# Attention with values as the stationary operand, and probabilities divided ahead of their transposes

## The chip, the cores and the metric

The kernel runs on one core of one Trainium2 chip. The metric is the device time of one execution in microseconds (us). The kernel before takes 1104.72 us, the median of three runs (1103.87 to 1105.32).

## The reference

A trunk of two layers over one sequence of 256 tokens of width 1024, in float32. Each layer is a feed-forward part, a token mixer and a second feed-forward part. Each part normalises its input, applies a shift and a scale, and adds its output times a gate; shift, scale and gate come from a conditioning vector through a large matrix (`ada_w`). The mixer of the first layer is attention with 16 heads, that of the second a state-space scan. The change lies in the attention:

```python
def one_block(args):
    q_blk, i = args
    s = jnp.einsum('bhqd,bhkd->bhqk', q_blk, kt) * scale
    q_pos = i * Q_BLOCK + jnp.arange(Q_BLOCK)
    s = jnp.where(k_pos[None, :] <= q_pos[:, None], s, -jnp.inf)
    p = jax.nn.softmax(s, axis=-1).astype(vt.dtype)
    return jnp.einsum('bhqk,bhkd->bhqd', p, vt)
```

Queries come in two blocks of 128 tokens, heads have 96 features for scores and 64 for values. The 16 results are joined to 1024 features and multiplied by `w_o`.

## The kernel before, in words

**Layout.** The state x lies with features on the 128 partitions (eight chunks of 128) and the 256 tokens along the free axis. A projection multiplies 128x128 pieces of weights (stationary) with 128x256 of tokens (moving). Weights come from HBM in float32 by DMAs of at most 2048 columns (`prefetch`, L171, issued on SP, five buffers `raw`). `split_next` (L200) splits each piece of 1024 columns into a high part (ScalarE, L197) and a low part (VectorE, L198), five pieces being held at most; `mm3` (L282) then does three passes of the rounded type fp32r. Every TensorE matmul is recorded at L272, every transpose at L277.

**The conditioning matrix.** `ada_w` comes over the same DMA queue, between the weights, in units of 1 MB. `plan` (L108) writes the order of all loads; `ADA_AT` says how many units lie in each of five parts (first feed-forward, attention, second, third, scan). `ada_half` (L229) takes the next loaded half unit, multiplies and sums it on VectorE (L236) and frees the buffer after the second half; it is called at fixed places (a call does nothing when no unit is loaded), and by `advance` when all buffers hold such units. The down projection (`down`, L442) of a feed-forward part calls it twice per output chunk.

**Attention** (`mla`, L693). The queries of each four heads (a quad) are projected, squared, rotated and transposed while earlier heads are being worked on. `turn(t)` (L947) works on several heads at once:

- `scores` (L869) of head t: the second block of queries against 256 keys and the first against 128, in plain float32, each followed by a bf16 matmul that adds the mask.
- `softmax` of head t-1: two maxima on VectorE (L887, L888), a small product (L889), two exponentials on ScalarE with their sums (L892).
- `probs_t` of head t-2: three 128x128 transposes on TensorE; `probs_evac` of head t-3 copies them to SBUF (VectorE L908, for one head in four ScalarE L906).
- `values` of head t-4: three float32 matmuls with the transposed probabilities stationary and 64 columns of values moving, so that the output has tokens on partitions.
- once per quad: `o_evac` divides by the sums (VectorE, L925 and L927), `o_t` transposes the result back to features on partitions (four transposes), `o_split` splits it (ScalarE L197, VectorE L198) for the projection by `w_o`.

Turns 0 to 18 stand ahead of that projection; turns 19 to 22 are called between the first pieces of it (`down`, two output chunks early, a hook after each two of the eight inputs).

**Order.** The program is handed to a planner (`tc`), which orders the instructions of each engine by its own costs and by what is ready in its plan; program order is kept only where `keep_in_program_order` says so. On the chip each engine then runs its list in that order.

## Time and profile before

| | us |
|---|---|
| median of the runs | 1104.72 |
| profiled execution | 1103.92 |
| its span | 1102.2 |
| TensorE busy | 1078.9 |
| VectorE busy | 864.9 |
| ScalarE busy | 610.7 |

The span is the stretch that the profile covers; the execution's own time is 1.72 us longer. A record of a matmul is longer than the distance to the next one, since matmuls are pipelined: the distance of two starts is what one costs. Attention with its turns lies from about 262 to 310 us.

### The profile page before, as it was taken

The page shows a single profiled execution, that of the slowest core. Times are in us where ns is not written, and L with a number is a line of the kernel's source. Part 1 is how long each engine was busy: PE and PEld are TensorE (multiplying, and loading weights), DVE is VectorE, ACT ScalarE, POOL GpSimd, SP SyncE. Part 2 cuts the span into 40 slices and gives each one's busy share as a digit, 9 for nine tenths or more (in the row PEclk, how much of TensorE's full clock was granted, in tenths as well). Part 3 has the DMA queues.
Part 4 walks back from the last instruction along what each step waited for, and adds up shares of the span by engine and source line. Part 5 has one row for each costly group of instructions (what it writes and reads, how often), then busy time and mean ns, then how long its engine had stood idle before and what let it go on. Part 6 is the DMA issues. An engine that isn't in the chain of part 4 may idle for free.

```text
span 1102.2 us, 21874 instructions
## 1 busy us (share of the span) xinstructions
PE 1078.9 (98%) x8890; PEld 1064.4 (97%) x8890; DVE 864.9 (78%) x1537; ACT 610.7 (55%) x1081; POOL 48.5 (4%) x107
## 2 busy tenths in 40 slices
PE   4999999999999999999999999999999999999998
PEld 3999999998999999999999999999999999999998
DVE  5889898789879988765999886598887777756642
ACT  4555444468757544444754444498678556544431
POOL 3000020010000000000000000000100100000000
PEclk9999999999999999999999999999999999999999
DMA  8988998755146888775689986544424355666630
GB/s 350 346 330 307 363 358 326 255 202 187 39 162 242 303 328 294 283 263 192 230 326 365 351 321 250 174 149 155 151 98 153 115 192 176 219 222 224 235 130 20
DMA packets 37400, 258.54 MB, mean 235 GB/s; under 512 B 4274, under 2 KB 5426, under 8 KB 6708
## 3 DMA queue, kind: packets, MB, share of 16 engines
q1 hardware_dynamic: 37300, 257.16, 63.7%
q8 instruction: 69, 1.13, 0.4%
q14 instruction: 31, 0.25, 0.1%
HBM read 256.10 MB, written 1.05 MB: 233 GB/s over the span
## 4 chain that ended last, share of the span: by engine, by line
PE 94%; DVE 2%; DMA 1%; ACT 1%; issue 1%; POOL 0%; SPq 0%; POOLq 0%; ACTq 0%
PE bank L272 93%; PE bank L277 2%; DMA raw<-in_adaw_dram 1%; DVE raw L236 1%; DVE wlo L198 1%; ACT whi L197 0%; ACT t L892 0%; DVE sl L307 0%; POOL t L1312 0%; SPq L328 0%; POOL sl L557 0%; POOL rr L415 0%; DVE sl L1230 0%; SPq L178 0%; DVE mod L250 0%
## 5 line engine op out<-in xcount | busy, mean ns | idle before, releaser
L272 PE MATMUL bank<-sl,whi 128*128 128x256 f32 (+1 forms) x5312 | 953.7, 283 | 4.5 <-ACT whi L197 4.5
L272 PEld LDWEIGHTS bank<-sl,whi 128*128 128x128 f32 x5312 | 815.9, 188 | 6.1 <-ACT whi L197 5.0
L272 PE MATMUL bank<-sl,wlo 128*128 128x256 f32 (+1 forms) x2656 | 746.6, 281 | 6.3 <-DVE wlo L198 6.2
L197 ACT CAST whi<-raw 128x1024 fp32r<-128x1024 f32 (+1 forms) x342 | 354.7, 1041 | 362.5 <-PE bank L272 261.7
L272 PEld LDWEIGHTS bank<-sl,wlo 128*128 128x128 f32 x2656 | 501.5, 189 | 7.2 <-DVE wlo L198 7.0
L198 DVE TENSOR_TENSOR wlo<-raw,whi 128x1024 fp32r<-128x1024 f32 (+1 forms) x342 | 412.9, 1212 | 118.2 <-ACT whi L197 116.5
L236 DVE SCALAR_TENSOR_TENSOR raw<-raw,cb 128x1024 f32<-128x1024 f32 x144 | 174.3, 1222 | 20.9 <-DMA raw<-in_adaw_dram 20.8
L306 ACT CAST sl<-t 128x256 fp32r<-128x256 f32 x125 | 48.9, 401 | 21.4 <-DVE t L490 15.5
L307 DVE TENSOR_TENSOR sl<-t,sl 128x256 fp32r<-128x256 f32 x125 | 51.3, 417 | 0.6 <-ACT sl L306 0.5
L435 DVE SCALAR_TENSOR_TENSOR x<-bank,mod,x 128x256 f32<-128x256 f32 x48 | 22.9, 480 | 28.1 <-PE bank L272 28.1
L490 DVE TENSOR_TENSOR t<-t,bank 128x256 f32<-128x256 f32 x70 | 29.2, 417 | 15.4 <-PE bank L272 15.4
L272 PE MATMUL bank<-sl,sl 128*128 128x64 f32 (+3 forms) x264 | 40.2, 291 | 0.0
L272 PEld LDWEIGHTS bank<-sl,sl 128*128 128x128 f32 (+1 forms) x264 | 34.4, 191 | 2.8 <-issue 0.5
L1035 DVE SCALAR_TENSOR_TENSOR sl<-t,cst,sl 128x256 f32<-128x256 f32 x72 | 35.4, 494 | 1.1 <-ACT sl L1033 0.6
L385 ACT ACTIVATE sl<-x,scol 128x256 fp32r<-128x256 f32 x40 | 20.3, 508 | 21.9 <-DVE x L435 21.7
L384 POOL CAST sl<-bspl 128x4 fp32r<-128x4 f32 x40 | 16.1, 446 | 303.8 <-PE bank L272 134.5
L489 ACT ACTIVATE t<-bank 128x256 f32<-128x256 f32 x70 | 26.3, 378 | 0.0
L415 POOL TENSOR_TENSOR rr<-rv,mhalf 128x2 f32<-128x2 f32 x12 | 10.9, 911 | 311.8 <-DVE rv L411 297.7
L272 PE MATMUL bank<-whi,sl 128*128 128x384 f32 (+1 forms) x80 | 24.3, 369 | 0.0
L386 DVE SCALAR_TENSOR_TENSOR sl<-x,scol,sl 128x256 fp32r<-128x256 f32 x40 | 19.1, 480 | 4.8 <-ACT sl L385 4.8
L398 ACT ACTIVATE t<-t,mod,scol 128x256 f32<-128x256 f32 x32 | 18.3, 596 | 6.7 <-DVE t L397 6.7
L1157 ACT ACTIVATE sl<-bank,nac 128x128 f32<-128x128 f32 x64 | 18.3, 373 | 4.3 <-PE bank L272 4.3
(207 smaller groups left out, 611.9 us busy)
## 6 DMA issues: line engine op xcount, KB each, us to landing
raw<-in_wgu_dram SPq DMA_DIRECT2D x88, 1024.0 KB, 5.4
raw<-in_adaw_dram SPq DMA_DIRECT2D x72, 1024.0 KB, 6.9
raw<-in_wdn_dram SPq DMA_DIRECT2D x44, 1024.0 KB, 6.3
raw<-in_win_dram SPq DMA_DIRECT2D x19, 1024.0 KB, 5.0
raw<-in_wout_dram SPq DMA_DIRECT2D x8, 1024.0 KB, 4.8
raw<-in_mwo_dram SPq DMA_DIRECT2D x4, 1024.0 KB, 4.9
raw<-in_mwq_dram SPq DMA_DIRECT2D x3, 768.0 KB, 4.2
raw<-in_mwa_dram SPq DMA_DIRECT2D x2, 1024.0 KB, 7.0
```

The source lines that it names most:

```text
L197: self.nc.scalar.copy(out=hi, in_=raw)
L198: self.nc.vector.tensor_tensor(out=lo, in0=raw, in1=hi.bitcast(F32), op=ALU.subtract)
L236: nc.vector.scalar_tensor_tensor(out=w, in0=w, scalar=1.0, in1=self.cb, op0=ALU.mult, op1=ALU.mult, accum_out=self.mod[:, q, 2 * u + i:2 * ...
L272: ins = self.nc.tensor.matmul(*a, **k)
L277: ins = self.nc.tensor.transpose(*a, **k)
L306: self.nc.scalar.copy(out=hi, in_=src)
L307: self.nc.vector.tensor_tensor(out=lo, in0=src, in1=hi.bitcast(F32), op=ALU.subtract)
L385: nc.scalar.activation(out=hi[:, 0:T], in_=self.x[m], func=AF.Copy, scale=sc)
L435: nc.vector.scalar_tensor_tensor(out=self.x[m], in0=ps[:, 0:T], scalar=self.mod[:, q, m:m + 1], in1=self.x[m], op0=ALU.mult, op1=ALU.add)
L489: nc.scalar.activation(out=tg, in_=pg[:, 0:T], func=AF.Silu)
L490: nc.vector.tensor_tensor(out=tg, in0=tg, in1=pu[:, 0:T], op=ALU.mult)
L1035: nc.vector.scalar_tensor_tensor(out=dst, in0=u[:, t:t + T], scalar=cw[:, t:t + 1], in1=dst, op0=ALU.mult, op1=ALU.add)
```

## The change

- `values` takes a pair of heads. The values (128 tokens by 64 features) are stationary and the transposed probabilities move. The two heads write to partitions 0 to 63 and 64 to 127 of one bank, as features by tokens, 256 columns wide. So `o_evac` and `o_t` go, and `o_split` splits one 128x256 result per pair.
- `norm` is new: as the division can no longer be made on the output, each head's probabilities are divided before their transposes: a reciprocal, a product of 128x256 on VectorE and one of 128x128 on ScalarE.
- `probs_t` puts its three blocks in another order in the bank.
- `scores` adds the mask to both blocks by one matmul of 256 columns.
- `ADA_AT` moves four units (4 MB) from the attention's loads to those of the first feed-forward part, whose down projection calls `ada_half` three times per output chunk.
- The turns end two earlier, at 20; turns 17 to 20 are called inside `down`.

```diff
--- before.py
+++ after.py
@@ -30,7 +30,7 @@
 NDEF = 6
 ZRAW = 13
 SETUP_AT = 15
-ADA_AT = (20, 4, 16, 20, 0)
+ADA_AT = (24, 0, 16, 20, 0)
 BIG_NEG = -1e30
 SSD_ORDER = "ccccczzcz" + "ccczccczz" + "ccczcccz" * 2 + "zzzzzz"
 SSD_STEPS = (1, 1)
@@ -536,7 +536,7 @@
             if not s or j > NDEF:
                 self.ada_half()
             prev = cur
-        self.down(s, NJ, lambda k: H[k], [lambda: evac(prev, None)], 2, 1, 2)
+        self.down(s, NJ, lambda k: H[k], [lambda: evac(prev, None)], 2, 1, 2 if s else 3)
 
     def open_first(self):
 
@@ -864,7 +864,7 @@
         QT[0] = [self.heads_evac(b, None) for b in qb]
         q_evac(1, 1, p1)
 
-        SC, PB, PTs, O, DEN, OT, ON, OB = {}, {}, {}, {}, {}, [], {}, {}
+        SC, PB, PTs, O, DEN, OT = {}, {}, {}, {}, {}, []
 
         def scores(h):
             quad, hh = divmod(h, 4)
@@ -873,14 +873,13 @@
             qt = QT[quad][i][0:96, j * 256:(j + 1) * 256]
             ps = SC[h] = self.bank()
             self.matmul(ps[:, 0:256], qt[:, 128:256], kt, start=True, stop=False)
-            self.matmul(ps[:, 128:256], self.identb, self.maskq, start=False, stop=True)
-            self.matmul(ps[:, 256:384], qt[:, 0:128], kt[:, 0:128], start=True, stop=False)
-            self.matmul(ps[:, 256:384], self.identb, self.maskq, start=False, stop=True)
+            self.matmul(ps[:, 256:384], qt[:, 0:128], kt[:, 0:128], start=False, stop=False)
+            self.matmul(ps[:, 128:384].rearrange("p (c l) -> p c l", c=2), self.identb,
+                        self.maskq.rearrange("p (o l) -> p o l", o=1).broadcast_to([128, 2, 128]),
+                        start=False, stop=True)
 
         def softmax(h):
             quad, hh = divmod(h, 4)
-            if hh == 0:
-                DEN[quad] = self.small([128, 2, 4], "den", 3)
             cq = CQ[quad]
             ps = SC[h]
             mx = self.small([128, 2], "mx", 4)
@@ -888,17 +887,25 @@
             nc.vector.reduce_max(out=mx[:, 0:1], in_=ps[:, 256:384], axis=AX.X)
             nc.vector.scalar_tensor_tensor(out=mx, in0=mx, scalar=-1.0, in1=cq[:, :, hh], op0=ALU.mult, op1=ALU.mult)
             P = self.t3()
+            den = DEN[h] = self.small([128, 2], "den", 4)
             for c, sl in ((1, slice(0, 256)), (0, slice(256, 384))):
                 nc.scalar.activation(out=P[:, sl], in_=ps[:, sl], func=AF.Exp, bias=mx[:, c:c + 1],
-                                     scale=cq[:, c, hh:hh + 1], accum_out=DEN[quad][:, c, hh:hh + 1])
+                                     scale=cq[:, c, hh:hh + 1], accum_out=den[:, c:c + 1])
             SC[h] = P
 
+        def norm(h):
+            P, den = SC[h], DEN.pop(h)
+            nc.vector.reciprocal(out=den, in_=den)
+            nc.vector.tensor_scalar(out=P[:, 0:256], in0=P[:, 0:256], scalar1=den[:, 1:2], scalar2=None, op0=ALU.mult)
+            nc.scalar.activation(out=P[:, 256:384], in_=P[:, 256:384], func=AF.Copy, scale=den[:, 0:1])
+
         def probs_t(h):
+
             P = SC.pop(h)
             pp = PB[h] = self.bank()
             for b in range(3):
-                self.transpose(out=pp[:, b * 128:(b + 1) * 128], in_=P[:, b * 128:(b + 1) * 128],
-                                    identity=self.ident)
+                o = (b + 1) % 3 * 128
+                self.transpose(out=pp[:, o:o + 128], in_=P[:, b * 128:(b + 1) * 128], identity=self.ident)
 
         def probs_evac(h):
             PTs[h] = self.t3()
@@ -907,42 +914,19 @@
             else:
                 nc.vector.tensor_copy(out=PTs[h], in_=PB.pop(h)[:, 0:384])
 
-        def values(h):
-            quad, hh = divmod(h, 4)
-            half, h8 = divmod(h, 8)
-            if hh == 0:
-                O[quad] = self.bank()
-            PT = PTs.pop(h)
-            hc = slice(h8 * 64, (h8 + 1) * 64)
-            o0 = O[quad][:, hh * 64:(hh + 1) * 64]
-            o1 = O[quad][:, 256 + hh * 64:256 + (hh + 1) * 64]
-            self.matmul(o1, PT[:, 0:128], V[0][half][:, hc], start=True, stop=False)
-            self.matmul(o1, PT[:, 128:256], V[1][half][:, hc], start=False, stop=True)
-            self.matmul(o0, PT[:, 256:384], V[0][half][:, hc], start=True, stop=True)
-
-        def o_evac(quad):
-            den = DEN.pop(quad)
-            nc.vector.reciprocal(out=den, in_=den)
-            t = ON[quad] = self.slot()
-            nc.vector.tensor_tensor(
-                out=t.rearrange("p (c h d) -> p c h d", c=2, d=64),
-                in0=O.pop(quad).rearrange("p (c h d) -> p c h d", c=2, d=64),
-                in1=den.rearrange("p c (h o) -> p c h o", o=1).broadcast_to([128, 2, 4, 64]), op=ALU.mult)
-
-        def o_t(quad):
-            t = ON.pop(quad)
-            ps = OB[quad] = self.bank()
-            for b in range(2):
-                for c in range(2):
-                    self.transpose(out=ps[:, b * 256 + c * 128:b * 256 + (c + 1) * 128],
-                                        in_=t[:, c * 256 + b * 128:c * 256 + (b + 1) * 128], identity=self.ident)
-
-        def o_split(quad):
-            ps = OB.pop(quad)
-            hi, lo = self.slot(F32R), self.slot(F32R)
-            self.split_pair(hi, lo, ps)
-            for b in range(2):
-                OT.append((hi[:, b * T:(b + 1) * T], lo[:, b * T:(b + 1) * T]))
+        def values(pair):
+
+            ps = O[pair] = self.bank()
+            hs = [2 * pair, 2 * pair + 1]
+            PT = [PTs.pop(h) for h in hs]
+            for c in range(2):
+                for j, h in enumerate(hs):
+                    half, h8 = divmod(h, 8)
+                    self.matmul(ps[j * 64:(j + 1) * 64, c * 128:T], V[c][half][:, h8 * 64:(h8 + 1) * 64],
+                                PT[j][:, c * 256:256 + c * 128], start=(c == 0), stop=(c == 1))
+
+        def o_split(pair):
+            OT.append(self.split_act(O.pop(pair)[:, 0:T]))
 
         def turn(t):
 
@@ -954,14 +938,14 @@
                     q_rstd(1)
                 if nq < 4:
                     turn.p0 = q_proj(nq, 0)
+            if 0 <= t - 2 < HEADS:
+                norm(t - 2)
             if 0 <= t - 3 < HEADS:
                 probs_evac(t - 3)
             if 0 <= t - 1 < HEADS:
                 softmax(t - 1)
-            if t >= 8 and t % 4 == 0:
-                o_evac(t // 4 - 2)
-            if t >= 10 and t % 4 == 2:
-                o_split(t // 4 - 2)
+            if t >= 6 and t % 2 == 0:
+                o_split(t // 2 - 3)
             if t < HEADS:
                 scores(t)
             if nq < 4:
@@ -974,10 +958,8 @@
                     q_rstd(nq)
             if 0 <= t - 2 < HEADS:
                 probs_t(t - 2)
-            if 0 <= t - 4 < HEADS:
-                values(t - 4)
-            if t >= 9 and t % 4 == 1:
-                o_t(t // 4 - 2)
+            if t >= 5 and t % 2 == 1:
+                values(t // 2 - 2)
             if quad + 1 < 4:
                 if hh == 1:
                     turn.qb = quad_t(QQ[quad + 1])
@@ -986,10 +968,10 @@
             if t % 2 == 1:
                 self.ada_half()
 
-        tail = HEADS + 3
+        tail = HEADS + 1
         for t in range(tail):
             turn(t)
-        rest = [lambda t=t: turn(t) for t in range(tail, HEADS + 7)]
+        rest = [lambda t=t: turn(t) for t in range(tail, HEADS + 5)]
         self.down(s, 8, lambda k: OT[k], rest, 2, 2, 1, MLA_EVERY)
 
 
```

## Rows read from the trace of the kernel before

**Rows 1.** The page, part 1: busy us, share of the span, instructions
```profile
PE 1078.9 (98%) x8890; PEld 1064.4 (97%) x8890; DVE 864.9 (78%) x1537; ACT 610.7 (55%) x1081; POOL 48.5 (4%) x107
```

**Rows 2.** The page, part 4: the chain that ended last, by engine
```profile
PE 94%; DVE 2%; DMA 1%; ACT 1%; issue 1%; POOL 0%; SPq 0%; POOLq 0%; ACTq 0%
```

**Rows 3.** Two windows: length, busy (x instructions) of PE, PEld, DVE, ACT, POOL; clock; DMA share; GB/s
```profile
262.00:274.00 12.00, 10.73 (x72) 9.45 (x71) 11.57 (x48) 9.68 (x27) 0.00 (x0) 1.00 0.67 240
...
262.00:298.00 36.00, 34.69 (x266) 31.46 (x265) 32.21 (x123) 28.89 (x91) 0.20 (x2) 1.00 0.33 118
```

**Rows 4.** Timeline of TensorE for one head: start us, us recorded, engine, line, operation
```profile
295.51 0.60 PE L272 MATMUL bank<-sl,sl 96*128 96x256 f32 x2
295.95 0.22 PE L272 MATMUL bank<-maskq,identb 128*128 128x128 bf16 x1
296.00 0.44 PE L272 MATMUL bank<-sl,sl 96*128 96x128 f32 x2
296.28 0.22 PE L272 MATMUL bank<-maskq,identb 128*128 128x128 bf16 x1
296.34 0.50 PE L277 MATMUL bank<-ident,t 128*128 128x128 f32 x3
296.67 0.78 PE L272 MATMUL bank<-sl,t 128*128 128x64 f32 x6
297.29 0.43 PE L272 MATMUL bank<-sl,sl 96*128 96x256 f32 x1
```

**Rows 5.** The chain of waits, 290 to 330: start us, us, what
```profile
301.10 0.82 PE bank L277 x7
305.17 0.44 PE bank L277 x4
```

**Rows 6.** Groups of VectorE by form: xcount | busy us, mean ns | idle before
```profile
L307 DVE TENSOR_TENSOR sl<-t,sl 128x256 fp32r<-128x256 f32 x125 | 51.3, 417 | 0.6 <-ACT sl L306 0.5
L887 DVE TENSOR_REDUCE mx<-bank 128x1 f32<-128x256 f32 x16 | 6.7, 418 | 2.0 <-PE bank L272 2.0
L888 DVE TENSOR_REDUCE mx<-bank 128x1 f32<-128x128 f32 x16 | 4.5, 280 | 0.0
L198 DVE TENSOR_TENSOR sl<-bank,sl 128x512 fp32r<-128x512 f32 x4 | 2.8, 690 | 2.6 <-ACT sl L197 2.6
L927 DVE TENSOR_TENSOR sl<-bank,den 128x512 f32<-128x512 f32 x4 | 2.8, 689 | 0.8 <-PE bank L272 0.8
L666 DVE TENSOR_SCALAR t<-t,bcol,cst 128x256 f32<-128x256 f32 x5 | 2.0, 410 | 0.0
L925 DVE RECIPROCAL den<-den 128x8 f32<-128x8 f32 x4 | 0.8, 196 | 0.6 <-ACT t L892 0.6
```

**Rows 7.** The groups of VectorE again, 262 to 298 only
```profile
L236 DVE SCALAR_TENSOR_TENSOR raw<-raw,cb 128x1024 f32<-128x1024 f32 x2 | 2.4, 1216 | 0.0
```

**Rows 8.** Groups of ScalarE by form
```profile
L306 ACT CAST sl<-t 128x256 fp32r<-128x256 f32 x125 | 48.9, 401 | 21.4 <-DVE t L490 15.5 <-DVE t L497 5.2 <-DVE t L666 0.5
L892 ACT ACTIVATE t<-bank,mx,cq 128x256 f32<-128x256 f32 x16 | 9.1, 570 | 4.5 <-DVE mx L889 4.5
L892 ACT ACTIVATE t<-bank,mx,cq 128x128 f32<-128x128 f32 x16 | 7.3, 458 | 0.0
L197 ACT CAST sl<-bank 128x512 fp32r<-128x512 f32 x4 | 2.4, 588 | 5.1 <-PE bank L277 5.1
L1180 ACT COPY t<-bank 128x128 f32<-128x128 f32 x4 | 1.0, 257 | 0.0
```

**Rows 9.** The same for 30 to 210, the first feed-forward part
```profile
30.00:210.00 180.00, 178.52 (x1500) 178.25 (x1499) 160.01 (x269) 87.69 (x134) 9.52 (x13) 1.00 0.87 328
```

**Rows 10.** Waits 30 to 222: who waited for whom, us, times, longest
```profile
ACT whi L197 <- PE bank L272: 52.4, 36, 2.4
```

**Rows 11.** Timeline of TensorE where 32-column weights begin
```profile
224.87 0.50 PE L272 MATMUL bank<-ones,ssum 128*128 128x1 f32 x4
225.23 0.41 PE L272 MATMUL bank<-sl,whi 128*32 128x258 f32 x2
```

## The prediction

> **What bounds the kernel now.** I read the page's busy times first. TensorE is busy for 98% of the span [rows 1], and the chain that ended last is TensorE's for 94% [rows 2]; the reader is to see that a microsecond of TensorE's work counts nearly everywhere, and work of other engines only where TensorE waits. The windows come next, since the shares are means. In the attention, 262 to 298, TensorE is busy for 34.69 of 36 us, VectorE for 32.21 and ScalarE for 28.89; nearly all of TensorE's idle time lies in the first 12 us (10.73 of 12), where VectorE is busy for 11.57 [rows 3]. So TensorE is the bound here, but VectorE stands right behind it, and the change takes work from the first and gives it to the second. The timeline of one head in the middle of the attention shows TensorE without a gap, one head in 1.78 us (295.51 to 297.29) [rows 4].
>
> **The change part by part, TensorE.** All costs are distances of two starts.
>
> The transposes of the output go: four per quad, 0.44 us for four [rows 5], four quads, 1.76 us.
>
> The mask. A head's scores take 0.83 us: 0.44 for the float32 pair of passes with 256 columns, 0.05 for a mask, 0.28 for the pair with 128, 0.06 for a mask [rows 4]. After the change the first pair stays at 0.44; the second takes between 0.22 (half of the first) and 0.28; one mask of 256 columns takes the two old ones together, 0.10 to 0.12. That is 0.76 to 0.84, so a head gains 0.07 or loses 0.01. I take 0.04, since the 0.28 holds 0.06 that a pair of 256 doesn't have per column and that I put down to the change of type: 0.6 us over 16 heads, between -0.2 and 1.1. The maxima now wait for the whole of the scores and not for their first part; that is 0.3 us later, a turn ahead of need.
>
> The values. Before, six passes of 64 columns take 0.62 us per head [rows 4], 0.10 each, though the columns alone would need a quarter of the 0.22 that 256 take: loading 128 columns of weights sets this pace, as it does for matmuls of a single column (four in 0.36) [rows 11]. After, a head has two passes of 256 and two of 128: 0.44 plus 0.22 to 0.28, so 0.66 to 0.72. One after the other that is 0.04 to 0.10 more per head. No row shows two matmuls in two halves of the columns. If the second pass of one head ran beside the first of the other, a pair would need 0.88 and not 1.32, a head 0.18 less than before. I take 0.05 more, because it needs only what rows 4 show: 0.8 us, between +1.6 and -2.9.
>
> TensorE in all: 1.76 + 0.6 - 0.8 = 1.6 us less, with ends at 0 and 5.8.
>
> **VectorE and ScalarE.** VectorE gets 16 reciprocals at 0.196, at most (the row has eight columns, the new ones two), 16 products of 128x256 at 0.410, and eight low parts of 128x256 at 0.417: 13.0 us. It loses four reciprocals at 0.196 and four divisions at 0.689, four low parts of 128x512 at 0.690 [rows 6], and two halves of the conditioning matrix at 1.22 [rows 7]: 8.7 us. Net 4.3 more. The nearest row for the product is L666, the same form in SBUF, at 0.410. ScalarE gets 16 products of 128x128, bounded by a plain copy at 0.257 and the exponential at 0.458; I take 0.36, halfway, 5.8 us; and eight high parts at 0.401, less four at 0.588 [rows 8]: 6.6 more.
>
> The row of the product is also where a rule speaks: 128 columns take 0.280 in the maximum and 256 take 0.418 [rows 6], so an element costs about 1.08 ns, and the product's 0.410 is that of a plain pass. The Trainium skill's page "VectorE: DVE Perf Modes", section "The perf-mode tier table (the rule you actually need)", says that a float32 `tensor_scalar` in SBUF runs at twice that rate. By the rule one product would take 0.27, an estimate (0.410 less the 0.138 of 128 columns), and VectorE's addition would be 2.2 us smaller, which would help the first rival below; the row disagrees.
>
> Put together for 262 to 298 [rows 3]: VectorE 32.2 + 4.3 = 36.5, ScalarE 28.9 + 6.6 = 35.5, TensorE 34.7 - 1.6 = 33.1. VectorE then has more work than the stretch is long, while some of its records overlap and the last heads reach past 298. So what TensorE saves inside the stretch is mostly not to be had: VectorE is late next. Past 298 the other engines have room: two of the four transposes of outputs lie there (at 301.10, among seven, and 305.17) [rows 5], 0.88 us, and I count them in full. Of the other 0.7 I count half. The sum is 1.2 us.
>
> **The new wait.** The reciprocal waits on VectorE for ScalarE's sums of the same head; behind it in the written order stand the product, the copy of the transposed probabilities of the head before and the maxima of the next head, for which ScalarE's exponentials wait. ScalarE's product waits for the reciprocal, and the transposes for both products. This ping-pong costs nothing where the planner puts other work between; the third rival has its price.
>
> **The moved loads.** Four units of 1 MB, each with a DMA on SP, two passes of 1.22 on VectorE with the read of their sum, go past the attention's weights into the first feed-forward part. From 30 to 210 us the DMA moves 328 GB/s at a share of 0.87, and VectorE is busy for 160.0 of 180 us [rows 9]. Four MB more in 180 us make 351 GB/s, a share of 0.93; eight passes at 1.3 make VectorE 170.4 at most. Both fit, and the weights are split well ahead: ScalarE waited 36 times, 52.4 us, for TensorE to free a piece [rows 10]. So I cost it at nothing. If that cover were gone, the price, an estimate, would be what a share held at 0.90 leaves over, 0.03 of 180 us, 5.4 us. In the attention the weights' loads come earlier by the same four DMAs, which frees time that the queue doesn't lack (a share of 0.33) [rows 3]. The two turns that move into `down` put the last heads' waits beside its matmuls; before, TensorE had no gap there either, so nothing is counted.
>
> The profiled execution took 1103.92 us, 1.72 over its span; 1.2 less is 1102.7. It lies 0.8 under the median of the runs, 1104.72, so I expect a median of 1103.5.
>
> **The rivals.** First: TensorE stays the bound and the halves run side by side. For it: rows 4 show no gap, and some VectorE records overlap; against it: VectorE's 36.5 us. TensorE would save 1.76 + 0.6 + 2.9 = 5.3; of this 0.88 and 1.1 (six heads past 298 at 0.18) count in full and half of the remaining 3.3, 3.6 in all: 1101.1 us. The Trainium skill's page "TensorEngine Tiling (Array Packing)", section "Key Properties", says that tiles work independently of each other, which would make this the case; no row of before shows it.
>
> Second, to the other side: each turn becomes a loop. If the planner leaves a head's division ahead of the next head's maxima, VectorE's maxima (0.418 + 0.280) are followed by ScalarE's exponentials (0.570 + 0.458), these by the reciprocal and the product (0.196 + 0.410) [rows 6, 8], and only then come the next maxima: 2.33 us, where a head takes 1.78 now. It decides from the point where this order stands in VectorE's list, and over the eight heads that have no query work to fill the gaps it costs 0.55 x 8 = 4.4: 1104.7 - 1.2 + 4.4 = 1107.9. For it speaks that ScalarE already waits for the product of the maxima, 4.5 us in all [rows 8]; against it that the planner reorders by what is ready.
>
> Third: going into and out of half-width weights empties TensorE's pipe. A mask is recorded for 0.22 where the next matmul starts 0.05 later, so an emptied pipe shows 0.17 [rows 4]; 16 times that, twice per pair, is 2.7 us: 1103.5 + 2.7 = 1106.2. Against it: four one-column matmuls, 0.36 us for four, are followed by weights of 32 columns without a gap [rows 11]. The page just named says, in the same section, that a change of the tiling mode empties the engine; the rows disagree as far as 32 columns at the first partition go.
>
> **How the numbers follow.** The forecast, VectorE as the new pace, has a chance of 0.42 and a range of its own of 1102 to 1105. The first rival has 0.28, the loop 0.18, the emptied pipe 0.12. The range reaches from 1100.6 to 1107.2: it leaves out some 0.06 of the first rival, where more than half of the 3.3 is had, and some 0.12 of the loop, where it is whole. Below 0.2%, which is 2.2 us, this kernel's runs can't be told from no change. Faster by more (under 1102.5) is the first rival and a small part of the forecast, 0.36; slower by more (over 1106.9) is the loop, 0.18; the rest, 0.46, is within.
>
> **What would show it.** In the trace after, the transposes of outputs are gone, a head's scores start 0.76 to 0.84 before its next work, and a pair's values take 1.3 (the forecast) or 0.9 (the first rival). VectorE should be busy for 34 us or more of 36 in the attention, and TensorE should have idle time there, ended by VectorE's or ScalarE's products. A wait of the reciprocal for the sums in every turn shows the loop; a gap ahead of each pair's values shows the emptied pipe. TensorE's windows from 30 to 210 should stay full; if they don't, the moved loads were not free and I am wrong there. A product at 0.27 would show that the row of L666 was the wrong one.

## The result, and the profile after

The kernel after takes 1112.68 us, the median of four runs (1110.69 to 1113.21), against 1105.02 for the kernel before beside it: a ratio of 1.0068, with an interval of 1.0054 to 1.0081. That is 7.5 us more. The forecast was 1103.5, its range ended at 1107.2: slower was the side with the smallest chance, and the size was missed. Four things share the time (the moved loads, a wait, the products' work and TensorE's clock); the experiments take them apart. Traced runs with a mean granted clock of 0.998 have a spell at half clock in their opening (39 to 43 us; 0.61 in e1, 1.00 in the kernel before), and a kernel's runs at 0.998 are about 1.5 us longer than its runs at 1.000 (before: 1105.5 and 1104.0), so some comparisons below are made at the same clock.

The page's busy line and its chain of waits of the kernel after answer to [rows 1] and [rows 2]:

```profile
PE 1077.7 (97%) x8826; PEld 1057.7 (95%) x8826; DVE 869.7 (78%) x1565; ACT 614.2 (55%) x1101; POOL 43.4 (4%) x107
...
PE 90%; DVE 5%; ACT 2%; DMA 1%; issue 1%; POOL 0%; SPq 0%; ACTq 0%; POOLq 0%
```

TensorE's busy time hardly moved (1078.9 before), but its share of the chain fell from 94 to 90%, while VectorE's rose from 2 to 5%: TensorE now waits. The windows of the attention, with the columns of [rows 3], and one short window behind it:

```profile
262.00:274.00 12.00, 11.27 (x80) 10.51 (x78) 11.61 (x49) 11.60 (x28) 0.00 (x0) 1.00 0.41 131
262.00:298.00 36.00, 29.94 (x211) 25.57 (x211) 33.27 (x134) 31.51 (x94) 0.00 (x0) 1.00 0.26 88
...
304.00:308.00 4.00, 4.00 (x18) 3.14 (x15) 1.56 (x6) 1.37 (x5) 0.10 (x1) 0.50 0.00 0
```

From 262 to 298 TensorE is busy for 29.94 us and not for 34.69, and yet the attention ends later. From 304 to 308 it shows as full, but at a granted clock of 0.50, that is, at 1.2 and not 2.4 GHz: a busy TensorE is no proof of speed there.

What the engine does when nothing is late shows in its timeline (columns as in [rows 4]):

```profile
281.86 0.49 PE L277 MATMUL bank<-ident,t 128*128 128x128 f32 x3
282.28 0.87 PE L272 MATMUL bank<-t,sl 128*64 128x256 f32 x8
283.08 1.08 PE L277 MATMUL bank<-ident,t 128*96 128x128 f32 x8
...
295.02 0.82 PE L272 MATMUL bank<-sl,sl 96*128 96x256 f32 x4
295.68 0.27 PE L272 MATMUL bank<-maskq,identb 128*128 128x256 bf16 x1
295.79 0.49 PE L277 MATMUL bank<-ident,t 128*128 128x128 f32 x3
296.12 0.82 PE L272 MATMUL bank<-sl,sl 96*128 96x256 f32 x4
...
296.89 0.63 PE L277 MATMUL bank<-ident,t 128*128 128x128 f32 x3
297.44 0.87 PE L272 MATMUL bank<-t,sl 128*64 128x256 f32 x8
298.24 0.92 PE L272 MATMUL bank<-sl,sl 96*128 96x256 f32 x4
```

A head's scores with the mask take 0.77 (295.02 to 295.79; 0.83 before), three transposes 0.33 as before, and the values of two heads 0.80 (297.44 to 298.24; twice 0.62 before): 1.50 a head where it was 1.78. So TensorE has less to do than the forecast thought, and the time is lost in waiting. One place, on all engines (the brackets give the idle time ahead and what ended it):

```profile
302.16 0.34 DVE L899 TENSOR_SCALAR t<-t,den 128x256 f32<-128x256 f32 x1
...
302.49 0.27 DVE L887 TENSOR_REDUCE mx<-bank 128x1 f32<-128x128 f32 x1
...
302.65 0.87 PE L277 MATMUL bank<-ident,t 128*128 128x128 f32 x3 [0.96 <-DVE den L898]
302.68 0.35 DVE L899 TENSOR_SCALAR t<-t,den 128x256 f32<-128x256 f32 x1
303.45 0.30 PEld L272 LDWEIGHTS bank<-t,sl 128*64 128x64 f32 x4 [0.33 <-issue]
303.45 1.55 PE L272 MATMUL bank<-t,sl 128*64 128x256 f32 x8
303.56 0.56 DVE L915 COPY t<-bank 128x384 f32<-128x384 f32 x1 [0.53 <-PE bank L277]
...
304.04 0.15 DVE L888 SCALAR_TENSOR_TENSOR mx<-mx,cq 128x2 f32<-128x2 f32 x1
```

TensorE's transposes wait 0.96 us for the division: they start at 302.65, behind the product of their head (302.16 to 302.50; the trace names the reciprocal that ends next). VectorE's list has the next head's product (L899, 302.68) and the copy (L915) between a later head's maxima (L887) and their small product (L888), which ScalarE's exponentials need; the copy itself waits for the transposes, and these waited for the product of 302.16. At the half clock the same eight passes then take 1.48 us (303.45 to 304.93, where the next scores begin) and not 0.80.

The new instructions, 255 to 325 us (columns as in [rows 6]; VectorE, then ScalarE):

```profile
L899 DVE TENSOR_SCALAR t<-t,den 128x256 f32<-128x256 f32 x16 | 5.6, 347 | 0.1
...
L898 DVE RECIPROCAL den<-den 128x2 f32<-128x2 f32 x16 | 2.5, 158 | 0.9 <-ACT t L892 0.9
...
L900 ACT ACTIVATE t<-t,den 128x128 f32<-128x128 f32 x16 | 6.6, 410 | 3.5 <-DVE den L898 3.3
```

And the moved loads: two windows of the first feed-forward part (columns as in [rows 3]), and the waits from 30 to 222 us (columns as in [rows 10]):

```profile
150.00:180.00 30.00, 29.70 (x252) 29.50 (x252) 26.61 (x40) 13.20 (x19) 4.11 (x6) 1.00 0.93 353
180.00:210.00 30.00, 28.57 (x239) 28.15 (x238) 27.08 (x45) 13.52 (x19) 0.00 (x0) 1.00 0.90 327
```

```profile
ACT sl L385 <- DVE x L435: 28.0, 7, 5.7
...
ACT whi L197 <- PE bank L272: 19.0, 15, 2.6
```

Before, TensorE was full in both windows; the second one was:

```profile
180.00:210.00 30.00, 30.00 (x257) 30.00 (x256) 24.37 (x38) 14.13 (x19) 0.00 (x0) 1.00 0.75 270
```

ScalarE's wait for free weight pieces, which stood for "split well ahead", fell from 52.4 us [rows 10] to 19.0. In its place ScalarE waits 28.0 us, with later splits behind it in its list, for VectorE's sum into x (L435), which waits for TensorE.

### The profile page after: what moved, and what is told of

The parts are those of the page before. It is cut to its first block, busy times and chain, and to the rows that moved or that the text cites. A ratio compares the mean times of both kernels' runs of the same rounds, so it can differ in the third digit from the quotient of the medians.

```text
span 1110.5 us, 21781 instructions
## 1 busy us (share of the span) xinstructions
PE 1077.7 (97%) x8826; PEld 1057.7 (95%) x8826; DVE 869.7 (78%) x1565; ACT 614.2 (55%) x1101; POOL 43.4 (4%) x107
## 4 chain that ended last, share of the span: by engine, by line
PE 90%; DVE 5%; ACT 2%; DMA 1%; issue 1%; POOL 0%; SPq 0%; ACTq 0%; POOLq 0%
PE bank L272 89%; DVE wlo L198 1%; DVE raw L236 1%; PE bank L277 1%; DMA raw<-in_adaw_dram 1%; ACT whi L197 1%; ACT t L892 0%; ACT sl L690 0%; DVE sl L307 0%; DVE t L899 0%; DVE t L915 0%; POOL t L1294 0%; ACT t L813 0%; ACT sl L688 0%; DVE mx L886 0%
## 5 line engine op out<-in xcount | busy, mean ns | idle before, releaser
L435 DVE SCALAR_TENSOR_TENSOR x<-bank,mod,x 128x256 f32<-128x256 f32 x48 | 22.9, 481 | 31.5 <-PE bank L272 31.5
L277 PE MATMUL bank<-ident,t 128*96 128x128 f32 (+2 forms) x116 | 17.9, 285 | 8.5 <-DVE t L899 3.2
L277 PEld LDWEIGHTS bank<-ident,t 128*96 128x96 f32 (+2 forms) x116 | 13.4, 138 | 12.1 <-PE bank L272 4.3
L384 POOL CAST sl<-bspl 128x4 fp32r<-128x4 f32 x40 | 11.1, 322 | 308.5 <-DVE bspl L258 120.5
```

What stands on the lines that cost most here:

```text
L277: ins = self.nc.tensor.transpose(*a, **k)
L435: nc.vector.scalar_tensor_tensor(out=self.x[m], in0=ps[:, 0:T], scalar=self.mod[:, q, m:m + 1], in1=self.x[m], op0=ALU.mult, op1=ALU.add)
```

## The experiments

Ratios are to the kernel before on the same chip, with 95% intervals; 0.0010 is 1.1 us. Each run's record also has its mean granted clock; "at the same clock" compares runs that show the same mean.

### Which half of the change

**e1_ada_only**: the kernel before with the moved loads alone.

```diff
-ADA_AT = (20, 4, 16, 20, 0)
+ADA_AT = (24, 0, 16, 20, 0)
...
-        self.down(s, NJ, lambda k: H[k], [lambda: evac(prev, None)], 2, 1, 2)
+        self.down(s, NJ, lambda k: H[k], [lambda: evac(prev, None)], 2, 1, 2 if s else 3)
```

> The kernel before with the moved loads alone (ADA_AT and three half units per output chunk). Theory A (both parts cost time on their own): 1107 to 1109, with TensorE idle between 170 and 200 us. Theory B (the moved loads carry the whole loss): 1111 or more. If the stretch from 170 to 200 was an accident of the attention's order: 1105.

**e2_attn_only**: the kernel after with these two lines as before.

> The changed attention with the old placing of the loads. Theory A: 1108 to 1110, TensorE idle in the attention as in the changed kernel. Theory B: 1105 or less. The forecast's sum without its moved loads: 1103.8.

**e4_mask_only**: the kernel before with the new mask alone.

```diff
-            self.matmul(ps[:, 128:256], self.identb, self.maskq, start=False, stop=True)
-            self.matmul(ps[:, 256:384], qt[:, 0:128], kt[:, 0:128], start=True, stop=False)
-            self.matmul(ps[:, 256:384], self.identb, self.maskq, start=False, stop=True)
+            self.matmul(ps[:, 256:384], qt[:, 0:128], kt[:, 0:128], start=False, stop=False)
+            self.matmul(ps[:, 128:384].rearrange("p (c l) -> p c l", c=2), self.identb,
+                        self.maskq.rearrange("p (o l) -> p o l", o=1).broadcast_to([128, 2, 128]),
+                        start=False, stop=True)
```

> The kernel before with the one mask matmul of 256 columns alone. By TensorE's records (0.77 instead of 0.83 per head, 16 heads) 1.0 us less: 1104.0. If TensorE isn't what a head waits for: 1105.0. The interval will hardly tell these apart; the trace's distance between a head's scores and its next matmul will.

Measured: e1 1106.8 us, 1.0020 [1.0011, 1.0029]; e2 1110.34 us, 1.0048 [1.0033, 1.0063]; e4 1103.34 us, 0.9988 [0.9978, 0.9997]. The loads cost 2.2 us, the attention 5.3, and these add up to the 7.5 of the whole; the mask alone gains 1.3.

### What the division costs

**e3_no_norm**: e2 without the two products, so the output stays undivided. **e5_norm_tiny**: e2 with the products over two columns, so the same chain of waits with less work; all but these columns stay undivided.

```diff
-            nc.vector.tensor_scalar(out=P[:, 0:256], in0=P[:, 0:256], scalar1=den[:, 1:2], scalar2=None, op0=ALU.mult)
-            nc.scalar.activation(out=P[:, 256:384], in_=P[:, 256:384], func=AF.Copy, scale=den[:, 0:1])
+            nc.vector.tensor_scalar(out=P[:, 0:2], in0=P[:, 0:2], scalar1=den[:, 1:2], scalar2=None, op0=ALU.mult)
+            nc.scalar.activation(out=P[:, 256:258], in_=P[:, 256:258], func=AF.Copy, scale=den[:, 0:1])
```

> As e2, but the two products that divide the probabilities are left out (the reciprocal stays, the output is not divided). If the division's work and its wait hold TensorE back: TensorE without gaps in most of the attention, and its saving of about 6 us comes through, 1098 to 1100. If something else holds it back (banks, order, the pair): within 2 us of e2.

> As e2, but each head's two products take 2 columns instead of 256 and 128 (the rest of the probabilities is not divided): the waits for the sums and for the reciprocal stay, the work goes. Leaving the products out altogether took 7.8 us off e2 (1110.3 to 1102.6). If the added waits cost it: 1108 to 1110. If the products' work on VectorE and ScalarE costs it: 1103 to 1104.

Two columns do not take the work away, as this expects. The groups of e5, 255 to 325 us (columns as in [rows 6]; VectorE, then ScalarE):

```profile
L899 DVE TENSOR_SCALAR t<-t,den 128x2 f32<-128x2 f32 x16 | 3.6, 222 | 0.2
...
L900 ACT ACTIVATE t<-t,den 128x2 f32<-128x2 f32 x16 | 4.9, 304 | 4.3 <-DVE den L898 2.4 <-DVE mx L888 1.9
```

So of 5.6 us of products on VectorE and 6.6 on ScalarE, two columns leave out 2.0 and 1.7.

**e8_deep**: e2 with one turn more between the products and the transposes (and all that follows). **e15_deep_tiny**: e8 with the tiny products of e5.

```diff
-            if 0 <= t - 2 < HEADS:
-                probs_t(t - 2)
+            if 0 <= t - 3 < HEADS:
+                probs_t(t - 3)
...
-        tail = HEADS + 1
+        tail = HEADS + 2
```

> As e2, with the transposes of a head one turn later than its division, and all that follows one turn later too: the same work, one turn more for the products. If TensorE loses time because it reaches the transposes before the products are there: 1104 to 1107. If VectorE and ScalarE simply have too much work: 1109 to 1111.

> The attention's change with old loads and one turn more between the products and the transposes, the products over 2 columns only (the probabilities stay undivided but for these). Full products without the extra turn cost 7.8 us over none, tiny ones 4.1, full ones with the extra turn 3.2. If the cost is a wait of the turn plus the products' own work, and the two add up: 7.8 less 3.7 for the work and 4.6 for the wait leaves nothing, 1102.3 to 1103.0. If the reciprocal's place in VectorE's list costs something whatever comes after it: 1104 to 1105.

| products | no extra turn | an extra turn |
|---|---|---|
| full | e2: 1110.34, 1.0048 [1.0033, 1.0063] | e8: 1105.79, 1.0002 [0.9992, 1.0011] |
| two columns | e5: 1106.67, 1.0019 [1.0009, 1.0028] | e15: 1102.32, 0.9974 [0.9963, 0.9985] |
| none | e3: 1102.56, 0.9984 [0.9975, 0.9994] | |

The division costs 7.8 us (e2 less e3). A turn more takes back 4.4 to 4.6 at either width: that is the wait. The two widths differ by 3.5 to 3.7 at either depth: that is the 2.0 and 1.7 us of work. So these are two costs that add, as e15's first theory had it; e3 and e5 lie outside both of their expected ranges.

The medians mix clocks, though. At a mean clock of 1.000, e3 takes 1102.3, e15 1102.2, e8 1103.9 (two runs each) and e5 1104.5 (one run); at 0.998, e3 takes 1103.8, e15 1103.7, e8 1105.4 and e2 1107.9 (one run). At the same clock, then, the wait costs 2.3 to 2.5 us, the work that two columns leave out 1.7, and the work that they keep nothing where an extra turn is there for it: e15 takes e3's time. The rest of the 7.8, some 3.7, is time at half clock, in the attention and in the opening.

What TensorE's transposes wait for from 262 to 310 us, in e2 and in e3 (before it was 1.3 us, for the exponentials, L892):

```profile
L277 PE MATMUL bank<-ident,t 128*128 128x128 f32 (+1 forms) x87 | 13.6, 285 | 9.1 <-DVE t L899 4.3 <-ACT t L900 2.1 <-DVE mx L888 1.7
...
L277 PE MATMUL bank<-ident,t 128*128 128x128 f32 (+1 forms) x90 | 14.8, 279 | 2.8 <-ACT t L892 2.4 <-ACT sl L688 0.4
```

Windows of e3 and of e8 (columns as in [rows 3]):

```profile
262.00:274.00 12.00, 11.49 (x80) 10.90 (x79) 11.81 (x44) 10.87 (x29) 0.00 (x0) 1.00 0.52 178
274.00:286.00 12.00, 10.63 (x68) 7.80 (x67) 11.71 (x46) 9.55 (x29) 0.00 (x0) 1.00 0.46 174
286.00:298.00 12.00, 11.14 (x80) 8.28 (x79) 9.29 (x43) 8.98 (x33) 0.00 (x0) 1.00 0.01 1
```

```profile
262.00:274.00 12.00, 9.84 (x70) 9.28 (x69) 11.82 (x46) 11.22 (x30) 0.00 (x0) 1.00 0.52 179
274.00:286.00 12.00, 11.51 (x82) 10.08 (x81) 11.47 (x54) 10.76 (x34) 0.00 (x0) 1.00 0.22 86
286.00:298.00 12.00, 9.59 (x69) 7.37 (x68) 11.04 (x47) 11.25 (x43) 0.00 (x0) 1.00 0.24 87
```

With an extra turn (e8), VectorE is busy for 11.04 to 11.82 of each 12 us, and TensorE still idles up to 2.4. That VectorE sets the pace there fits that 2.0 us of its products cost 1.7; ScalarE's 1.7 went with them, and no run separates the two. Even with no product at all (e3) VectorE is busy for 11.71 to 11.81 up to 286 (9.29 behind it), and TensorE's saving of 0.28 a head is mostly not to be had: e3 is 0.8 us below the mask alone (e4), no more than two runs of one kernel may differ. That VectorE is the reason there is not shown: e15, with an extra turn, gives it 3.5 us more to do and takes the same time.

### The clock

**e6_fill**: e2 with eight bf16 matmuls of 128 columns ahead of each head's transposes, into a free part of their bank; nothing reads them. They add 128 times 0.05 us [rows 4], 6.4 us of work for TensorE.

```diff
             pp = PB[h] = self.bank()
+            for _ in range(8):
+                self.matmul(pp[:, 384:512], self.identb, self.identb, start=True, stop=True)
```

> As e2, with eight bf16 matmuls of 128 columns ahead of each head's transposes, into columns that nobody reads: 0.43 us of TensorE work per head, 6.8 in all, where TensorE idled for 9.1 us in the attention. If half of the lost time is the half clock that follows idle stretches: no stretch at the lower clock in the attention and 1107 to 1109. If the clock is a side effect: the same as e2 or slower, 1110 to 1113.

Measured: 1107.45 us, 1.0021 [1.0011, 1.0030]: 2.9 us less than e2, with more work. Two windows of e2, then of e6 (the column behind the five engines is the clock):

```profile
274.00:286.00 12.00, 11.32 (x70) 10.01 (x68) 10.34 (x43) 8.88 (x30) 0.00 (x0) 0.86 0.22 87
286.00:298.00 12.00, 9.48 (x59) 7.09 (x59) 10.31 (x43) 9.68 (x31) 0.00 (x0) 0.86 0.24 87
```

```profile
274.00:286.00 12.00, 12.00 (x110) 10.29 (x108) 10.81 (x49) 10.54 (x33) 0.00 (x0) 1.00 0.17 69
286.00:298.00 12.00, 12.00 (x115) 10.12 (x113) 11.12 (x47) 10.76 (x40) 0.00 (x0) 1.00 0.13 38
```

In e2 the clock falls in both windows, behind idle time of TensorE (9.16 busy of the 12 us before); in e6 TensorE is never idle in these and keeps 2.4 GHz. The one run of e2's four at a mean clock of 0.998 took 1107.9, as e6's at that clock (1107.9, five runs); the other three, at 0.993 to 0.995, took 1110.1 to 1110.6. So, as far as one run can tell, some 2.5 of e2's 5.3 us are time at half clock. Not every idle stretch brings it: e8 has 9.59 of 12 at a clock of 1.00.

### The order of VectorE's work, and another engine

**e7_order** and **e12_deep_order**: e2 and e8 with a head's softmax written ahead of the division of the head before it. **e10_deep_pool**: e8 with both products on GpSimd.

```diff
-            if 0 <= t - 2 < HEADS:
-                norm(t - 2)
...
             if 0 <= t - 1 < HEADS:
                 softmax(t - 1)
+            if 0 <= t - 2 < HEADS:
+                norm(t - 2)
```

```diff
-            nc.vector.tensor_scalar(out=P[:, 0:256], in0=P[:, 0:256], scalar1=den[:, 1:2], scalar2=None, op0=ALU.mult)
-            nc.scalar.activation(out=P[:, 256:384], in_=P[:, 256:384], func=AF.Copy, scale=den[:, 0:1])
+            nc.gpsimd.tensor_scalar(out=P[:, 0:256], in0=P[:, 0:256], scalar1=den[:, 1:2], scalar2=None, op0=ALU.mult)
+            nc.gpsimd.tensor_scalar(out=P[:, 256:384], in0=P[:, 256:384], scalar1=den[:, 0:1], scalar2=None, op0=ALU.mult)
```

> As e2, with the maxima of head t-1 written ahead of the division of head t-2 in each turn. If the loop of my second rival stands because the division comes first on VectorE: 1106 to 1108. If the planner's order doesn't hang on it: 1110.

> As e8, with the maxima written ahead of the division. e7 took about 1 us off e2 this way. If both mend the same wait: 1105.5 to 1106, no gain over e8. If they add: 1104.5.

> As e8 (one turn more between division and transposes), with both products of a head on GpSimd, which is idle there, instead of VectorE and ScalarE. If their work is what is left to pay in e8 (VectorE busy for 11.0 to 11.8 of 12 us): 1101 to 1103. If GpSimd takes so long that the transposes wait for it, or slows VectorE down: 1106 or more.

Measured: e7 1109.16 us, 1.0040 [1.0025, 1.0055]; e12 1106.57 us, 1.0014 [1.0005, 1.0024]; e10 1108.56 us, 1.0028 [1.0018, 1.0038]. The written order gains nothing that can be told from e2 and loses about 1 us on e8, 2.1 at the same clock; both runs lie outside their expected ranges. That the division's place ahead of the maxima is what costs is not borne out. GpSimd takes nearly three times as long as VectorE for the larger product (groups of GpSimd, 255 to 325, columns as in [rows 6]):

```profile
L899 POOL TENSOR_SCALAR t<-t,den 128x256 f32<-128x256 f32 x16 | 15.9, 994 | 34.4 <-ACT t L815 23.4 <-DVE den L898 10.9
L900 POOL TENSOR_SCALAR t<-t,den 128x128 f32<-128x128 f32 x16 | 11.2, 700 | 0.0
```

At 1.69 us for the two, a head's division is longer than TensorE's whole head (1.50), so the transposes wait again.

### What in the moved loads costs time

**e11_ada_hook2**: e1 without the third call per output chunk.

> As e1 (moved loads, kernel before otherwise), but with two half units per output chunk of the down projection as before, not three. e1 lost 2.2 us where VectorE worked without a break from 174 to 191 us. If the third half unit on VectorE is what costs: 1104.5 to 1105.5. If the 4 MB on the DMA queue cost: 1107.

**e13_ada_narrow** and **e16_ada_last**: e1 with eight half units multiplied over 16 columns and not 1024 (the conditioning lacks the rest): in e13 units spread over the part, in e16 the last four (`q == 6`). **e14_ada_twice**: the kernel before, its loads unmoved, with one more pass over eight half units. **e17_ada_thin**: e16, and these four units are also loaded as 32 columns.

```diff
+            n = 16 if u == 1 and q in (3, 4, 5, 7) else D
-            nc.vector.scalar_tensor_tensor(out=w, in0=w, scalar=1.0, in1=self.cb, op0=ALU.mult, op1=ALU.mult,
+            nc.vector.scalar_tensor_tensor(out=w[:, :n], in0=w[:, :n], scalar=1.0, in1=self.cb[:, :n], op0=ALU.mult,
```

```diff
+            if u == 1 and q in (3, 4, 5, 7):
+                nc.vector.scalar_tensor_tensor(out=w, in0=w, scalar=1.0, in1=w, op0=ALU.mult, op1=ALU.max)
```

```diff
+            n = 32 if u[0] == "a" and u[1] == 6 else src.shape[-1]
-            self.nc.sync.dma_start(out=raw[:, :src.shape[-1]], in_=src)
+            self.nc.sync.dma_start(out=raw[:, :n], in_=src[:, :n])
```

> The loads of the conditioning matrix moved as in the change (24 units in the first part, none in the attention) on the kernel before, but eight half units of the first part are multiplied and summed over 16 columns instead of 1024 (the conditioning then lacks the rest of them). So VectorE has its old work in the first part, and the DMA queue has the 4 MB more. If VectorE's eight passes cost the 1.7 to 2.2 us of the moved loads: 1105.0 to 1105.5, as before. If the 4 MB on the queue cost them: 1106.8 still.

> The kernel before with its old loads, but eight half units of the first part get one more pass of VectorE over 1024 columns (it leaves the data as it is). The counterpart: VectorE's work without the DMA's. If VectorE's passes cost the moved loads' 2 us: 1107.0. If the DMA does: 1105.2, with VectorE busier by 9.7 us between 30 and 210 and TensorE as before. An answer between the two says that it takes both.

> As e13, but the eight half units that are multiplied over 16 columns only are the last four units loaded in the first part, which with moved loads VectorE works off between 174 and 191 us, where it never rests and TensorE waits for it; in e13 the narrowed ones lay earlier and that stretch stayed as it was. If VectorE's passes in that place are the cost: TensorE is full from 150 to 210 (60 of 60 us, with 58.26 in e13) and the time is 1105.0 to 1105.5. If the 4 MB on the queue are: 58.3 again and 1106.5.

> As e16, and the last four units of the first part are also loaded as 32 columns instead of 2048 (the rest of them is left out of the conditioning): neither the bytes nor VectorE's passes of the moved units are left, but each still takes one of the five load buffers from its issue to its pass. If the bytes on the queue cost the moved loads' time: 1105.0 to 1105.5, TensorE full from 150 to 210. If it is the buffers that they hold, or the order of the splits that the planner writes around them: 1106.5 or more. For the buffers speaks that with moved loads a load lands 4.9 us after its issue, 7.4 before: the queue is not crowded, the issue is late.

| | median us | ratio | at clock 0.998, against before |
|---|---|---|---|
| e1: moved | 1106.8 | 1.0020 [1.0011, 1.0029] | +1.3 |
| e11: moved, two calls | 1106.77 | 1.0015 [1.0005, 1.0024] | +1.5 |
| e13: moved, passes narrowed | 1106.55 | 1.0009 [1.0000, 1.0018] | +1.4 |
| e16: moved, the last passes narrowed | 1106.77 | 1.0014 [1.0005, 1.0023] | +1.4 |
| e14: unmoved, passes added | 1104.34 | 0.9993 [0.9985, 1.0002] | +0.5 |
| e17: moved, passes and bytes taken away | 1103.47 | 0.9990 [0.9981, 0.9999] | -0.8 |

It isn't the third call, and it isn't VectorE's time: taking its passes away leaves the 1.4 us, adding them does nothing that can be measured. With the bytes gone, the cost is gone, and e17 lies below both of its expected ranges. My guess with e17, that the load buffers which the units hold cost the time, is not settled by it: e17 takes the same buffers, but holds each for 6 to 10 us from its load's issue to its first pass, where e16 holds them for 10 to 15. A window of e16, one of e17 (columns as in [rows 3]):

```profile
180.00:210.00 30.00, 28.56 (x238) 28.13 (x238) 18.97 (x45) 13.43 (x19) 0.00 (x0) 1.00 0.90 347
```

```profile
180.00:210.00 30.00, 30.00 (x256) 30.00 (x255) 21.78 (x42) 14.37 (x19) 0.00 (x0) 1.00 0.81 302
```

In e16 VectorE has a third of the window free and TensorE still stands for 1.44 us, as in the kernel after. The timelines of ScalarE, VectorE and TensorE in e16 show where (its lines are one further on: x is summed at L436, matmuls are at L273):

```profile
190.92 0.51 ACT L386 ACTIVATE sl<-x,scol 128x256 fp32r<-128x256 f32 x1 [4.97 <-DVE x L436]
...
191.64 3.87 ACT L197 CAST whi<-raw 128x1024 fp32r<-128x1024 f32 x4
...
193.67 0.50 PE L273 MATMUL bank<-sl,whi 128*128 128x256 f32 x2 [0.44 <-ACT whi L197]
...
199.00 0.48 DVE L436 SCALAR_TENSOR_TENSOR x<-bank,mod,x 128x256 f32<-128x256 f32 x1 [3.74 <-PE bank L273]
199.40 2.35 DVE L198 TENSOR_TENSOR wlo<-raw,whi 128x1024 fp32r<-128x1024 f32 x2
...
200.67 0.39 PE L273 MATMUL bank<-sl,wlo 128*128 128x256 f32 x1 [1.00 <-DVE wlo L198]
```

TensorE's two waits, 0.44 and 1.00, are for splits that stand in a list behind work on x, and x waits for TensorE: ScalarE idles 4.97 us ahead of its splits, VectorE 3.74 ahead of its own. The loads were there: from 165 to 202 us no engine of e16 waits for a DMA. So the queue does not deliver late; the lists, which the planner wrote with the 4 MB in them, hold the splits back. What in the planner's costs makes it write them so is open: a hand-written order with the loads in place wasn't tried.

The moved loads also give something back. The start of the attention in e1:

```profile
262.00:274.00 12.00, 12.00 (x90) 11.27 (x88) 11.52 (x47) 11.60 (x32) 0.00 (x0) 1.00 0.36 121
```

TensorE had 10.73 of 12 there [rows 3]. So the first part loses more than the net 1.4, and e17, which has this gain too (12.00) without the loss, ends below the kernel before. Whether the earlier weights bring the gain, or the two halves of the conditioning matrix that VectorE no longer has there [rows 7], isn't separated.

### Where the new form has room

**e9_hybrid** and **e18_hybrid_quad**: old loads, the new mask, and the new form with the extra turn for heads 8 to 15 (e9) or 12 to 15 (e18) alone, the others as before.

```diff
+        NEW = 12
...
+            if NEW <= t - 2 < HEADS:
+                norm(t - 2)
...
+            if t >= NEW + 6 and t % 2 == 0:
+                values2(t // 2 - 3)
```

> Heads 0 to 7 as before, heads 8 to 15 as changed with the extra turn of e8, the one mask matmul for all, the old loads. The query work ends with head 7, and VectorE is busy for 9.75 of 12 us behind it before. If room on VectorE decides whether TensorE's saving comes through: four pairs at 0.44 and two output transposes of four at 0.44 and the mask, some 3 us in all: 1102 to 1103. If the division holds TensorE up even there: 1104 to 1105.

> As e9, with old loads and one mask for both blocks, but only the last quad (heads 12 to 15) takes the new values and the division ahead of its transposes, with the extra turn. There VectorE has no query work, so the division should lie beside other work, and the four transposes of that quad and two of the four turns inside the output projection's hooks go. If what the hybrid gains over the mask alone comes from these last heads: 1102.5. If the new form has nothing to give even there: 1103.3, as the mask alone.

Measured: e9 1103.2 us, 0.9984 [0.9975, 0.9993]; e18 1102.58 us, 0.9982 [0.9973, 0.9991]. Both beat the kernel before and the kernel after (e9 lies between its two expected ranges); against the mask alone (0.9988) neither can be told apart, and at the same clock e18 and e4 agree within 0.2 us. Two windows of e18, then the second one of e4:

```profile
286.00:298.00 12.00, 11.96 (x98) 11.38 (x96) 10.30 (x37) 9.79 (x34) 0.20 (x2) 1.00 0.01 1
298.00:310.00 12.00, 10.88 (x88) 9.48 (x89) 6.77 (x17) 5.72 (x16) 1.70 (x16) 1.00 0.01 2
...
298.00:310.00 12.00, 12.00 (x106) 11.90 (x106) 6.45 (x15) 5.17 (x14) 1.78 (x16) 1.00 0.01 2
```

TensorE is full up to 298 in e18, but the heads there are still nearly all of the old form: the first new product starts at 295.95. Where the new heads lie, TensorE stands for 1.1 of 12 us, though VectorE has room (6.77 of 12); with the mask alone it stands for none. So what the new form saves goes into waits there too, and e18's 1102.58, close to the 1102.5 of its first theory, shows no gain of these heads.

## Why the prediction was wrong

**The moved loads** are the first step that failed: costed at nothing, they cost 2.2 us (1.2 to 3.2), 1.4 at the same clock, with a gain in the attention already in it. The step summed means over 180 us; 351 GB/s at a share of 0.93 were expected, and 340 at 0.91 came. But the cover it named, weights split well ahead, did not hold: the wait that stood for it went from 52.4 us to 19.0, and splits now stand behind work on x in their engines' lists, while their loads are in time (e16). The wait is a rough gauge at that, since it is 23.8 in e17, where little is lost. A cover is no constant: it belongs to the loads and the lists of before.

**The new wait** is the second. It was costed at nothing "where the planner puts other work between". It costs 4.4 us (e5 less e15, the same work), 2.3 at the same clock. (The price that the prediction points at is its second rival's, the loop, not the third's.) I judged whether VectorE and ScalarE would wait; the place that waits is TensorE, for the product. It has less to do per head, so it reaches the transposes sooner, two turns after the scores as before, but with the reciprocal and the products in between.

**The products' work** is the third. VectorE was put at 36.5 of 36 us, and this only capped the gain. It should have cut both ways: work beyond an engine's room costs time. Of 5.6 us of products on VectorE, 3.6 cost nothing once a turn is there for them (e15 beside e3); the last 2.0, with ScalarE's 1.7, cost 1.7 at the same clock (e8 less e15), 3.5 by the medians. In the kernel after itself VectorE shows 33.27 of 36 us, under the 34 that the prediction named as its sign: it waits as well. And past 298 us, where the forecast counted its saving in full, TensorE, full before (6.00 of 6 us to 304), is busy for 3.91.

**The clock** was in no step. A wait of TensorE was priced at its length; in this kernel stretches at half clock follow, worth some 2.5 us in e2 (one run). They are part of what the medians give for the wait and the products above, not beside it.

**TensorE's own terms.** The transposes went as forecast. The mask gives 0.06 a head and not 0.04, 1.0 us, where e4 measured 1.3. The values went past the other end of the bounds (2.9): a pair takes 0.80 and not 1.32, since the two halves run side by side, so 3.5 us are saved where 0.8 more were counted. The Trainium skill's page "TensorEngine Tiling (Array Packing)", section "Key Properties", says that tiles work independently of each other; the trace now agrees. It gained little here, as the forecast said of any TensorE saving in this stretch: e3 lies 0.8 us below the mask alone. That VectorE is the next bound fits e8 (busy for 11.04 to 11.82 of 12), and it was the wrong comfort.

**The rivals.** The first had its mechanism (the halves) and not its time. The second had the right side, 1107.9, with a loop through VectorE and ScalarE. Its sign, the reciprocal waiting for the sums in every turn, isn't there (0.9 us over 16), and the order it turned on is worth nothing that e7 could show: the loop that costs runs through TensorE's transposes. The third expected 0.17 at each change of width; three transposes ahead of values take 0.42 at the least (281.86 to 282.28) where they take 0.33 ahead of scores, and a pair takes 0.80 where two beside each other would need 0.66 to 0.72. So some 0.2 a pair may be of that kind, 1.5 us; no run separates it.

**The small prices.** The product took 0.347: neither the 0.410 of L666, whose form has one scalar operand more, nor the 0.27 estimated by the rule of the Trainium skill's page "VectorE: DVE Perf Modes", section "The perf-mode tier table (the rule you actually need)". The rate does agree with that page: from 2 columns (0.222, e5) to 256 (0.347) it is 0.49 ns an element, about half of the 1.08 of a plain pass; what the estimate had too small is the part that doesn't grow with the columns, 0.22 and not 0.13. ScalarE's took 0.410, not 0.36. Neither decided anything.

## What to carry to other kernels

When an engine is nearly full, price the part of new work that goes beyond its room at its whole length, and not only as a limit on the gain; and ask of a new step what the bounding engine itself waits for, a turn ahead, before asking whether the helpers wait. A cover read from the trace of before belongs to the loads and lists of before: work out what it becomes, and where TensorE then waits, see whether the data was late or only the place in an engine's list. A saving on TensorE that comes with idle time can cost clock as well as time, so look at the granted clock in short windows before reading "busy".

## What the hardware showed that I had not expected

- Two float32 matmuls with weights of 64 columns in the two halves of the array run side by side: 0.80 us for the eight passes of a pair, 1.32 one after the other by the prices of before.
- Adding 6.4 us of matmuls that nobody reads made a kernel 2.9 us faster (e6): TensorE stayed at 2.4 GHz, and at the same mean clock the two kernels take the same time (one run of e2).
- A float32 product of 128x256 in SBUF with one scalar per partition takes 0.347 us on VectorE and 0.994 on GpSimd; of 128x128, 0.410 on ScalarE and 0.700 on GpSimd. With two columns it still takes 0.222 on VectorE and 0.304 on ScalarE, so a product narrowed to two columns is not an experiment without the product's work.
